# Differential attention: squares written to a small SBUF tile, scaling and turn of seven heads one step later

## The chip, the core and the metric

The kernel runs on one core of one Trainium2 chip. The metric is the device time of one execution in microseconds (us), the median over repeated runs. Five engines matter: TensorE (PE, matmuls and transposes; PEld is its weight load), VectorE (DVE), ScalarE (ACT), GpSimd (POOL) and SyncE (SP, which issues most DMAs).

## What is computed

A trunk of two decoder layers on 512 tokens of width 1024. Each layer is a half-step SwiGLU feed-forward block, a token mixer, a cross-attention into 256 memory tokens and a second feed-forward block, each followed by a layer norm. The mixer of layer 0 is differential attention; only this stage is touched by the change. Cut to its core:

```python
q, k, v = split(x @ w_qkv, 3)          # 8 heads; q, k: two maps of 64; v: 128 wide
q, k = rope(q), rope(k)
for each head, each block of 128 queries:
    p = softmax(mask(q[c] @ k[c].T * 64**-0.5))   for c in (0, 1)
    o = (p[0] - lam * p[1]) @ v
o = o * rsqrt(mean(o**2, axis=-1) + eps) * subln_g * (1 - lam_init)
return o @ w_o
```

The mean of squares in the next-to-last line runs over the 128 values of one head and one token.

## The kernel before

**Precision.** Products are formed from pairs of tiles, a rounded high part and the low rest, so most products are three matmuls (`mm3`) and most results are split in two by ACT (copy, high part) and DVE (subtract, low part).

**Two strands.** `diff_attention` weaves two generators. `da_main` projects queries, keys and values head by head and ends with the first half of the output projection (`to_tokens` over heads 0 to 3). `da_side` runs the attention itself in steps: with 4 blocks of 128 queries (`NT`) and 8 heads there are 32 pairs (head h, block i), and step s = 4h + i starts pair (h, i). `weave` hands out units of the side between matmuls of the main strand: each unit has a weight (`W_SC`, `W_T`, `W_O`, `W_E`), and the next unit comes once matmuls worth 900 ns (`GAP`) times the weight of the one before have been put out. When the main strand has ended, the rest of the side follows without matmuls of the main strand in between; then the second half of the output projection runs.

**One step.** In step s the side does, in this order:

- `da_scores` for the pair of step s: four matmuls into two PSUM tiles (one for each map, 128 x 128(i+1)), then on DVE the masked minimum (L1076) and on ACT the exponential with its sum (L1079), both at high priority. Called SC.i below.
- `da_mix` for the pair one step back (DVE, L1088 to L1090), which joins the two maps.
- `da_turn` for the pair two steps back: i+1 transposes on PE into one PSUM tile (L489), split on ACT and DVE (L120, L121). Called T.i.
- `da_out` for the pair three steps back: the product with v into the PSUM tile `po` (L1111, L1112). Called O.i. Two blocks share one `po` tile, which is taken at O.0 or O.2 and read out after O.1 or O.3: ACT copies one part of it to `o` (L1117), DVE adds the other (L1118), and ACT squares the two blocks of `o`, summing each row into `sq` (L1121). The squares themselves are of no use; they are written back into the `po` bank. After O.3 POOL turns the sums into the factors `f` (L1128 to L1131).
- `da_scale` (ACT, L1137: four instructions on `o`), five steps after the head's last pair (`LS` = 5), and one step later `da_turn_out`: four transposes of `o` on PE (L489, `pt<-ident,o`) and a split into `oT` on ACT (L125) and DVE (L126). Called scale and turn-out.

So in the steady state a head's scale stands in step SC.0 of the head two further on, after T.2 and O.1 of the next head, and its turn-out in the step SC.1, after T.3 and O.2 and ahead of SC.2.

**PSUM.** Besides the two tiles of the projections (`mm`), six banks serve the side: three tags (px, py, yz) of two buffers each. `aux` hands the tags out in rotation, one call after another. A cycle of four steps makes 15 calls, a multiple of three: in order SC.0 (two), T.2, SC.1 (two), T.3, the `po` tile of O.2 and O.3, turn-out, SC.2 (two), T.0, SC.3 (two), T.1, the `po` tile of O.0 and O.1. So every third of these shares two buffers: the second tile of SC.3, for one, has the same tag as the second tile of SC.2 and the `po` tile of O.2.

**Order.** Each engine runs its instructions in an order fixed when the program is built. On PE it is here the order of the strands. On the other engines an instruction can stand ahead of its place in the text where its operands were expected earlier.

Of the kernel before, what the change touches and what calls it, by code (L numbers as in the profile page):

```python
# [12 lines left out]
AF = mybir.ActivationFunctionType  # L13
# [4 lines left out]
P = 128  # L18
D = 1024
S = 512  # L20
NT = S // P
# [7 lines left out]
DA_H = 8  # L29
# [7 lines left out]

V_FIRST, LEAD, GAP = 6, 6000, 900
W_SC, W_T, W_O, W_E = (1.1, 1.4, 1.8, 2.2), (0.5, 0.7, 0.9, 1.1), (0.4, 0.8, 0.6, 1.1), (0.6, 0.8)
LM, LT, LO, LS = 1, 2, 3, 5  # L40
HALVES = (slice(0, DA_DK), slice(DA_DK, P))

FFN_TURNS = (((0, 1, 2), ()), ((3, 4), (0, 1)), ((5, 6), (2, 3)), ((7, 8), (4, 5)), ((9, 10), (6, 7)))
# [66 lines left out]
class Trunk:  # L110
# [75 lines left out]
    def mm(self, name):  # L186
        return self.mmp.tile([P, S], F32, tag="mm", name=name)
# [914 lines left out]
    def da_out(self, st, i):  # L1102
        nc = self.nc
        if i == 0:
            st["o"], st["sq"] = self.tmp("o", (P, NT, P)), self.small("sq", (P, NT))
        if i % 2 == 0:
            st["po"] = self.aux("po").rearrange("p (i s e) -> p i s e", i=2, s=2)
        a, o, po, mm = st.pop(("a", i)), st["o"], st["po"], nc.tensor.matmul
        for j in range(i + 1):
            v = st["v"][j][:, st["h"] % 2]  # L1110
            mm(po[:, i % 2], a[0][:, j], v, start=j == 0, stop=False)  # L1111
            mm(po[:, i % 2, 0], a[1][:, j], v[:, 0], start=False, stop=j == i)  # L1112
        if i % 2 == 0:
            return
        o2 = o[:, i - 1 : i + 1]
        with self.tc.high_priority():
            nc.scalar.copy(o2, po[:, :, 1])  # L1117
            nc.vector.tensor_tensor(o2, o2, po[:, :, 0], ALU.add)  # L1118
        sq = st["sq"]
        for i in range(i - 1, i + 1):  # L1120
            nc.scalar.activation(  # L1121
                po[:, 0, 0], o[:, i], AF.Square, scale=float(P**-0.5), accum_out=sq[:, i : i + 1]
            )
        if i < NT - 1:
            return

        f, G, s0 = self.small("f", (P, NT)), nc.gpsimd, st["sm"][:, :, 0]
        G.tensor_scalar(f, s0, EPS, None, ALU.mult)  # L1128
        G.tensor_tensor(f, f, s0, ALU.mult)
        G.tensor_tensor(f, f, sq, ALU.add)  # L1130
        G.tensor_tensor(f, f, self.mhalf, ALU.pow)  # L1131
        st["f"] = f
# [40 lines left out]
    def da_side(self):  # L1173

        n = DA_H * NT
        for s in range(n + LS + 2):
            h, i = divmod(s, NT)
            if s < n:
                while h >= len(self.heads) or self.clock < self.heads[h][0] + LEAD:
                    yield WAIT  # L1180
                self.da_scores(self.heads[h][1], i)
                yield W_SC[i]
            h, i = divmod(s - LM, NT)
            if 0 <= s - LM < n:
                self.da_mix(self.heads[h][1], i)
            h, i = divmod(s - LT, NT)
            if 0 <= s - LT < n:
                self.da_turn(self.heads[h][1], i)
                yield W_T[i]
            h, i = divmod(s - LO, NT)  # L1190
            if 0 <= s - LO < n:
                while len(self.heads[h][1]["v"]) < NT:
                    yield WAIT
                self.da_out(self.heads[h][1], i)
                yield W_O[i]
            h, i = divmod(s - LS, NT)
            if 0 <= s - LS < n and i == NT - 1:
                self.da_scale(self.heads[h][1])
                yield W_E[0]
            h, i = divmod(s - LS - 1, NT)  # L1200
            if 0 <= s - LS - 1 < n and i == NT - 1:
                self.oT[h] = self.da_turn_out(self.heads[h][1])
                yield W_E[1]

    def diff_attention(self, layer, ln):
        self.low_keys = [self.pair("low") for i in range(2)]
# [367 lines left out]

    def mixer(self, layer, ln):
        if layer == 0:
            bufs = dict(low=4, rt=2, a=4, p=6, o=2, qk=8, _x=0, v=4, oT=11, mask=1)
            with self.other_pools(), self.phase_pool(("v", "v"), "rt", **bufs):
                self.diff_attention(layer, ln)
            self.close_side()  # L1580
        else:
            self.later = ExitStack()
            self.later.enter_context(self.stage_pools(4, dict(raw=2), ("wh", "wl", "mem", "p", "raw")))
            self.to_w(self.later)
            self.kvp = self.later.enter_context(self.pool("kv"))
            bufs = dict(p=4, pw=1, gb=2, _x=0, pooled=16, sq=1)
            with self.phase_pool(("gb", "gb"), "sq", **bufs):
                side = self.pool_mixer(layer, ln)
                with self.tc.high_priority():
                    self.load_memory()  # L1590
                w = self.a["xa_wkv"][layer]
                raws = [self.raw_cols(w, c) for c in (0, D)]
                self.pool_bias()
                next(side)
                self.kv, self.keys, self.kv_bufs = [], [], 10
                self.weave(self.early_kv(layer, ln, 2, raws), side, 850, 8500)
            self.close_side()
# [46 lines left out]
```

## Time and profile before

| | us |
|---|---|
| median of 3 runs (lowest, highest) | 1926.35 (1923.81, 1928.33) |
| the profiled execution, its own time | 1925.08 |
| span of that execution | 1923.3 |
| PE busy | 1892.8 (98%) |
| DVE busy | 1563.6 (81%) |
| ACT busy | 1023.1 (53%) |
| POOL busy | 319.7 (17%) |

The span runs from the first to the last instruction that the profiler recorded; the execution's own time has 1.78 us more around it. Differential attention lies between about 335 and 570 us of the span, the part with the side strand between 371 and 563 us. A line of the profile's timeline gives start, duration, engine, line of the kernel, operation and operands, and in brackets the idle time of the engine just before and what ended it. In a list of waits the three numbers are the total, how many times, and the longest.

### The profile page before, as it was taken

Reading aid. Unit: us, or ns where it says so; the run is one execution under the profiler, and the core shown is the slowest. Engines: PE = TensorE matmul, PEld = TensorE weight load, DVE = VectorE, ACT = ScalarE, POOL = GpSimd, SP = SyncE. Lnnn points to the kernel's source line nnn. Section 1 sums busy time; section 2 is a strip of 40 time slices with the busy share of each in tenths; the row PEclk is TensorE's granted clock in tenths of the full one; section 3 lists DMA queues with packets and bytes.
Section 4 is the critical chain, followed back from the end, with each engine's and each line's share of the span. In section 5 each row is a group of like instructions: output and inputs, shape, how many; then the busy total and the mean of one; then the engine's idle time right before and its main releaser. Section 6 shows DMA issues by size and latency. Waiting matters only on the chain.

```text
span 1923.3 us, 32450 instructions
## 1 busy us (share of the span) xinstructions
PE 1892.8 (98%) x13050; PEld 1737.6 (90%) x13050; DVE 1563.6 (81%) x2263; ACT 1023.1 (53%) x1580; POOL 319.7 (17%) x278
## 2 busy tenths in 40 slices
PE   8999999999999999999999999999999999999998
PEld 7999998888878888999998999999899889999997
DVE  6888989888967558889888988898787568898886
ACT  6555554567755435645554655455455436555553
POOL 2112121111210001221220311212130012111210
PEclk9999999999999999999999999999999999999999
DMA  9978772322124317977785587778334337877861
GB/s 237 221 169 187 166 148 77 91 66 88 61 94 154 110 66 193 181 179 162 144 194 175 108 179 166 179 163 184 111 132 132 132 88 160 173 170 168 185 133 55
DMA packets 246742, 277.94 MB, mean 145 GB/s; under 512 B 8256, under 2 KB 212544, under 8 KB 246592
## 3 DMA queue, kind: packets, MB, share of 16 engines
q0 software_dynamic: 92928, 92.29, 31.2%
q1 hardware_dynamic: 153664, 183.59, 29.3%
q8 instruction: 102, 1.67, 0.4%
q14 instruction: 48, 0.39, 0.1%
HBM read 273.75 MB, written 2.10 MB: 143 GB/s over the span
## 4 chain that ended last, share of the span: by engine, by line
PE 78%; DVE 13%; ACT 4%; DMA 2%; issue 2%; POOL 1%; SPq 0%; DVEq 0%; ACTq 0%; POOLq 0%
PE x L205 7%; PE x L206 7%; PE x L207 7%; PE z L207 4%; PE z L206 4%; PE z L205 4%; PE ps L205 4%; PE ps L207 4%; PE ps L206 4%; DVE wl L121 2%; PE px L205 2%; PE px L207 2%; PE px L206 2%; DMA ra<-in_ffn_w_in_dram 2%; PE y L207 2%
## 5 line engine op out<-in xcount | busy, mean ns | idle before, releaser
L666 POOL DMA_DIRECT2D ra<-in_ffn_w_in_dram x132 | 170.8, 1317 | 987.0 <-DVE wl L121 802.6
L120 ACT CAST wh<-ra 128x1024 fp32r<-128x1024 f32 x184 | 193.4, 1053 | 216.7 <-PE x L206 68.1
L121 DVE TENSOR_TENSOR wl<-ra,wh 128x1024 fp32r<-128x1024 f32 x184 | 223.7, 1221 | 72.8 <-ACT wh L120 72.2
L120 ACT CAST wh<-rc 128x1024 fp32r<-128x1024 f32 x136 | 143.0, 1053 | 116.9 <-PE x L206 41.6
L205 PE MATMUL x<-xe,wh 128*128 128x256 f32 x704 | 195.0, 277 | 0.0
L206 PE MATMUL x<-xe,wh 128*128 128x256 f32 x704 | 194.8, 277 | 0.0
L207 PE MATMUL x<-xe,wl 128*128 128x256 f32 x704 | 194.8, 277 | 0.0
L121 DVE TENSOR_TENSOR wl<-rc,wh 128x1024 fp32r<-128x1024 f32 x136 | 164.8, 1221 | 28.2 <-ACT wh L120 27.8
L120 ACT CAST wh<-b 128x1024 fp32r<-128x1024 f32 x112 | 117.8, 1052 | 128.3 <-PE x L206 65.6
L121 DVE TENSOR_TENSOR wl<-b,wh 128x1024 fp32r<-128x1024 f32 x112 | 136.9, 1222 | 39.4 <-ACT wh L120 39.1
L205 PE MATMUL x<-xh,wh 128*128 128x256 f32 x544 | 151.1, 278 | 0.0
L206 PE MATMUL x<-xl,wh 128*128 128x256 f32 x544 | 150.6, 277 | 0.0
L207 PE MATMUL x<-xh,wl 128*128 128x256 f32 x544 | 150.6, 277 | 0.0
L206 PEld LDWEIGHTS x<-xe,wh 128*128 128x128 f32 x704 | 132.5, 188 | 1.4
L205 PEld LDWEIGHTS x<-xe,wh 128*128 128x128 f32 x704 | 132.2, 188 | 1.3
L207 PEld LDWEIGHTS x<-xe,wl 128*128 128x128 f32 x704 | 132.2, 188 | 0.0
L121 DVE TENSOR_TENSOR wl<-raw,wh 128x1024 fp32r<-128x1024 f32 x64 | 82.8, 1298 | 42.9 <-ACT wh L120 42.2
L206 PEld LDWEIGHTS x<-xl,wh 128*128 128x128 f32 x544 | 102.5, 188 | 0.7
L205 PEld LDWEIGHTS x<-xh,wh 128*128 128x128 f32 x544 | 102.1, 188 | 0.7
L207 PEld LDWEIGHTS x<-xh,wl 128*128 128x128 f32 x544 | 102.2, 188 | 0.0
L207 PE MATMUL y<-xh,wl 128*128 128x256 f32 x352 | 98.5, 280 | 1.2 <-DVE wl L121 0.5
L205 PE MATMUL z<-xh,wh 128*128 128x256 f32 x352 | 97.6, 277 | 1.2 <-ACT xh L120 0.8
(429 smaller groups left out, 6265.7 us busy)
## 6 DMA issues: line engine op xcount, KB each, us to landing
ra<-in_ffn_w_in_dram POOLq DMA_DIRECT2D x132, 512.0 KB, 6.9
rc<-in_ffn_w_in_dram SPq DMA_DIRECT2D x88, 512.0 KB, 5.7
b<-in_ffn_w_out_dram SPq DMA_DIRECT2D x76, 512.0 KB, 4.7
ra<-in_ffn_w_in_dram SPq DMA_DIRECT2D x44, 512.0 KB, 5.0
rc<-in_ffn_w_in_dram POOLq DMA_DIRECT2D x44, 512.0 KB, 7.6
raw<-in_xa_wkv_dram SPq DMA_DIRECT2D x16, 1024.0 KB, 5.5
raw<-in_da_w_qkv_dram SPq DMA_DIRECT2D x16, 512.0 KB, 5.2
raw<-in_xa_wq_dram SPq DMA_DIRECT2D x8, 1024.0 KB, 5.2
```

Source lines behind the costliest of these rows:

```text
L120: self.nc.scalar.copy(hi, src),
L121: self.nc.vector.tensor_sub(lo, src, hi.bitcast(F32)),
L205: mm(out, w[0], x[0], start=start, stop=False, skip_group_check=again)
L206: mm(out, w[0], x[1], start=False, stop=False, skip_group_check=again)
L207: self.last_mm = mm(out, w[1], x[0], start=False, stop=stop, skip_group_check=again)
L666: nc.gpsimd.dma_start(t, source(*block), accum_op=ALU.add)
```

## The change

It has two parts. In `da_out` ACT writes the squares to a new SBUF tile `squares` (128 x 128, one buffer) and not into the first block of the `po` bank; the sums still go to `sq`. In `da_side` the distance `LS` becomes a pair: 6 steps for heads 0 to 6 and 5, as before, for head 7. So scale and turn-out of seven heads move one step on. With the turn-out its call for a PSUM tile moves in the rotation; the order of a cycle becomes SC.0 (two), T.2, SC.1 (two), T.3, `po` of O.2, SC.2 (two), T.0, turn-out, SC.3 (two), T.1, `po` of O.0. The loop loses its last step, in which nothing was done; the count of instructions stays the same.

```diff
-LM, LT, LO, LS = 1, 2, 3, 5
+LM, LT, LO, LS = 1, 2, 3, (6, 5)
...
-        sq = st["sq"]
+        sq, squares = st["sq"], self.tmp("squares", (P, P))
         for i in range(i - 1, i + 1):
             nc.scalar.activation(
-                po[:, 0, 0], o[:, i], AF.Square, scale=float(P**-0.5), accum_out=sq[:, i : i + 1]
+                squares, o[:, i], AF.Square, scale=float(P**-0.5), accum_out=sq[:, i : i + 1]
             )
...
         n = DA_H * NT
-        for s in range(n + LS + 2):
+        for s in range(n + LS[1] + 1):
...
-            h, i = divmod(s - LS, NT)
-            if 0 <= s - LS < n and i == NT - 1:
-                self.da_scale(self.heads[h][1])
-                yield W_E[0]
-            h, i = divmod(s - LS - 1, NT)
-            if 0 <= s - LS - 1 < n and i == NT - 1:
-                self.oT[h] = self.da_turn_out(self.heads[h][1])
-                yield W_E[1]
+            for h in range(DA_H):
+                e = s - (h * NT + NT - 1 + LS[h == DA_H - 1])
+                if e == 0:
+                    self.da_scale(self.heads[h][1])
+                    yield W_E[0]
+                if e == 1:
+                    self.oT[h] = self.da_turn_out(self.heads[h][1])
+                    yield W_E[1]
...
-            bufs = dict(low=4, rt=2, a=4, p=6, o=2, qk=8, _x=0, v=4, oT=11, mask=1)
+            bufs = dict(low=4, rt=2, a=4, p=6, o=2, qk=8, _x=0, v=4, oT=11, mask=1, squares=1)
```

## The prediction

> **What bounds the kernel now.** I read the head of the page first, then PE's busy time in the stretch of the side strand (365 to 565 us), then the list of PE's waits in 335 to 575 us.
>
> ```profile
> span 1923.3 us, 32450 instructions
> PE 1892.8 (98%) x13050; PEld 1737.6 (90%) x13050; DVE 1563.6 (81%) x2263; ACT 1023.1 (53%) x1580; POOL 319.7 (17%) x278
> 365.00:565.00 200.00, 192.89 (x1141) 166.78 (x1139) 170.30 (x428) 133.91 (x360) 35.16 (x47) 1.00 0.25 79
> PE pt L489 <- DVE p L1090: 2.6, 2, 1.4
> PE sc L1070 <- ACT po L1121: 1.5, 2, 0.8
> PE pt L489 <- ACT o L1137: 1.1, 1, 1.1
> PE sc L1070 <- ACT qk L1057: 0.9, 2, 0.7
> PE po L1112 <- DVE a L121: 0.6, 1, 0.6
> ```
>
> PE is busy for 98% of the span. In this stretch (length, then busy time of PE, PEld, DVE, ACT, POOL) it stands still for 200 - 192.89 = 7.1 us, and the five lines below account for 6.7 of that. So no rearrangement of the side strand can win more than about 7 us, 0.37% of the kernel, and 1.4 of that is the longer of two waits for L1090, at the first head, before any scale or turn-out. What an edit to DVE or ACT is worth is only what it takes off these waits, or adds to them. They lie here:
>
> ```profile
> 416.21 0.33 PE L1070 MATMUL sc<-qk 128*128 128x128 f32 x1 [0.65 <-ACT qk L1057]
> 440.81 0.33 PE L1112 MATMUL po<-v,a 128*128 128x128 f32 x1 [0.64 <-DVE a L121]
> 485.77 0.33 PE L1070 MATMUL sc<-qk 128*128 128x128 f32 x1 [0.78 <-ACT po L1121]
> 489.10 0.55 PE L489 MATMUL pt<-ident,p 128*128 128x128 f32 x3 [1.21 <-DVE p L1090]
> 499.07 0.44 PE L1070 MATMUL sc<-qk 128*128 128x384 f32 x1 [0.68 <-ACT po L1121]
> 560.77 0.33 PE L489 MATMUL pt<-ident,o 128*128 128x128 f32 x1 [1.11 <-ACT o L1137]
> ```
>
> The 485.77 and 499.07 rows are SC.0 and SC.2 of head 5, waiting for a bank in which ACT still writes squares. The 560.77 row is the turn-out of head 7, when the main strand has run out.
>
> **Part 1: squares to SBUF.** No instruction is removed or added; 32 squares change their target, and a `po` bank is free after DVE's add (L1118) instead of after the second square (L1121). Around 485 us ACT and DVE ran as follows.
>
> ```profile
> 479.23 0.69 ACT L125 ACTIVATE oT<-pt,subg 128x512 fp32r<-128x512 f32 x1
> 479.81 0.61 ACT L1079 ACTIVATE p<-p,mx 128x384 f32<-128x384 f32 x1
> 481.14 0.17 DVE L1088 RECIPROCAL rc<-sd 128x1 f32<-128x1 f32 x1 [0.44 <-ACT p L1079]
> 484.06 0.41 DVE L1118 TENSOR_TENSOR o<-o,po 128x256 f32<-128x256 f32 x1
> 485.33 0.26 ACT L1121 ACTIVATE po<-o 128x128 f32<-128x128 f32 x1
> 487.14 0.40 ACT L1137 ACTIVATE o<-o,f 128x128 f32<-128x128 f32 x1 [0.77 <-POOL f L1131]
> 487.45 0.71 ACT L1079 ACTIVATE p<-p,mx 128x512 f32<-128x512 f32 x1
> 494.03 0.41 DVE L1118 TENSOR_TENSOR o<-o,po 128x256 f32<-128x256 f32 x1
> 498.62 0.28 ACT L1121 ACTIVATE po<-o 128x128 f32<-128x128 f32 x1
> ```
>
> With the bank free at 484.47 (484.06 + 0.41) PE need not wait at 485.77 - 0.78 = 484.99; with the second bank free at 494.44 it need not wait at 498.39. Upper bound: 0.78 + 0.68 = 1.46 us won. But the first wait is followed 3.3 us later by the 1.21 at 489.10 for DVE (L1090), and a PE that comes 0.78 earlier waits there so much longer, unless DVE comes earlier too. So the first is worth between 0 and 0.78; which, part 2 says. The second has no later wait behind it until the end of the stage: 0.68.
>
> The squares themselves get longer. Their rows and the nearest ones with the same 128 x 128 shape and an SBUF target:
>
> ```profile
> L1121 ACT ACTIVATE po<-o x32: 259/282/283, 392.2 to 558.4; 128x128 f32<-128x128 f32 x32
> L1137 ACT ACTIVATE o<-o,f x32: 385/392/406, 405.1 to 561.2; 128x128 f32<-128x128 f32 x32
> ```
>
> 392 - 282 = 0.11 us each (bounds: 0, if the target does not matter, and 0.11); I take 0.11. All 32 make 3.5 us of ACT time. ACT is busy for 133.91 of 200 us here, so 66 us of idle time hide it, except at the tail, where PE waits for a chain through two squares: 2 x 0.11 = 0.22 lost. Without that cover the 3.5 us would be the cost (a rival below). [...]
>
> **Part 2: scale and turn-out one step later.** I followed the units of the side strand through the weave by their weights. Scale and turn-out together weigh 1.4, that is 1.26 us of main-strand matmuls: SC.1, T.3, O.2, and then SC.2, T.0, O.3 of each cycle come up to that much earlier against the projections; SC.3 and all behind it stay. At the end, O.3 of head 7 now precedes the turn-out of head 6.
>
> The scale itself will hardly move. At 487.14 the first scale of head 3 ran on ACT before the exponentials of SC.3 of head 5 (487.45), some three units ahead of its place in the text: it is put where ACT would otherwise be idle, once `f` is expected. One step later in the text its place in that gap stays, so the wait for POOL (0.77 here) stays too. I cost this move at 0; the bounds are 0 and what the first rival wins.
>
> The turn-out does move on PE, and with it L125 (0.69) and L126. At 479.23 L125 runs just before the exponentials that DVE waits for at 481.14 (0.44 idle). Behind SC.2 it no longer delays them, so DVE reaches L1090 up to 0.44 earlier, and of the first 0.78 I count 0.44. Sum of the two PSUM waits: 0.44 + 0.68 = 1.1 us won (bounds 0.68 and 1.46).
>
> At the tail:
>
> ```profile
> 554.92 0.60 PE L489 MATMUL pt<-ident,o 128*128 128x128 f32 x4
> 556.05 0.28 PE L1111 MATMUL po<-v,a 128*128 128x256 f32 x1
> 557.11 0.38 ACT L1117 COPY o<-po 128x256 f32<-128x256 f32 x1 [0.87 <-PE po L1112]
> 560.31 1.28 ACT L1137 ACTIVATE o<-o,f 128x128 f32<-128x128 f32 x4 [1.49 <-POOL f L1131]
> ```
>
> O.3 of head 7 begins at 556.05, one group of three matmuls and the turn-out (from 554.92) later than it could: 1.1 us. ACT waited for it (0.87). Put ahead, the chain copy, add, squares, `f`, scale starts about 1.0 earlier, less 0.22 for longer squares: 0.8 of the 1.11 at 560.77 (bounds 0, if DVE's adds and the turn-out of head 6 get in between, and 1.11).
>
> The move has a price in banks. The second tile of SC.3 shares two buffers with its tag's last two tiles. Those were the second tile of SC.2 and `po` of O.2; now they are the tile of T.0, only one step old, and `po`, read out by the add after O.3. For heads 2, 4 and 6 the rows give the second SC.3 tile on PE, the DVE split of T.0 and the add:
>
> ```profile
> 432.38 0.50 PE L1070 MATMUL sc<-qk 128*128 128x512 f32 x1
> 433.37 0.29 DVE L121 TENSOR_TENSOR a<-pt,a 128x128 fp32r<-128x128 f32 x1
> 434.36 0.41 DVE L1118 TENSOR_TENSOR o<-o,po 128x256 f32<-128x256 f32 x1
> ...
> 481.16 0.40 PE L1070 MATMUL sc<-qk 128*128 128x512 f32 x1
> 482.45 0.28 DVE L121 TENSOR_TENSOR a<-pt,a 128x128 fp32r<-128x128 f32 x1
> ...
> 524.67 0.40 PE L1070 MATMUL sc<-qk 128*128 128x512 f32 x1
> 525.13 0.28 DVE L121 TENSOR_TENSOR a<-pt,a 128x128 fp32r<-128x128 f32 x1
> 525.34 0.41 DVE L1118 TENSOR_TENSOR o<-o,po 128x256 f32<-128x256 f32 x1
> ```
>
> At these times the split ends 1.28, 1.57 and 0.74 us after PE wants the bank: 3.6 us. T.0 comes up to 1.26 earlier, which leaves 0.02 + 0.31 + 0. I take 0.3 (bounds 0 and 3.6). Queued behind a waiting SC.3 tile are the projections, since PE keeps its order: such a wait is lost in full. I found no other tile that is late for its successor in the new rotation. The new SBUF tile lies behind the others of its stage, so no address of another tile moves. Queues of DMAs are not passed: neither part issues one, and POOL's four instructions per head stay behind O.3.
>
> **Sum.** -1.1 - 0.8 + 0.3 = -1.6 us. Against the profiled execution's 1925.08 that is 1923.5; that execution lay 1.27 below the median of the runs, so as a median 1926.35 - 1.6 = 1924.7 us.
>
> **Rivals.**
>
> First, the scale does come off the wait for `f`. Then heads 1 to 6 no longer hold ACT, and behind it DVE:
>
> ```profile
> ACT o L1137 <- POOL f L1131: 7.8, 7, 2.3
> 405.07 0.40 ACT L1137 ACTIVATE o<-o,f 128x128 f32<-128x128 f32 x1 [2.32 <-POOL f L1131]
> 407.46 0.42 DVE L121 TENSOR_TENSOR a<-pt,a 128x256 fp32r<-128x256 f32 x1 [2.16 <-ACT a L120]
> ```
>
> DVE would win some 2 us at 407, and the waits at 416 (0.65 and 0.20), 440.81 (0.64) and the rest of 489.10 (0.8) would go: 2.3 more, -3.9 in all, 1922.4 us. For it: ACT waits there 7 times, 7.8 us in all. Against it: the scale stands ahead of its place already.
>
> Second, slower: the bank of the second SC.3 tile decides. If the tile is given the `po` bank, PE waits for the add: 2.39 (432.38 to 434.77), 3.31 (481.16 to 484.47) and 1.08 (524.67 to 525.75), 6.8 us for three heads, net -1.9 + 6.8 = +4.9, 1931.2 us; with the tile of T.0 at the old times it is +1.7, 1928.0. It decides once T.0 and O.3 do not come earlier on DVE along with PE: their splits are queued on a DVE that is busy for 170.30 of 200 us, and the turn-out's split is now queued between. Against it: the high priority of the splits and of the add. [...]
>
> Third, the 3.5 us of longer squares fall on the path: squares stand before exponentials on ACT, for which DVE waits (481.14). Net +1.9, 1928.2 us.
>
> Fourth, nothing comes of it: the freed banks only move the two waits to DVE's L1090 and to a split, and the tail keeps its wait: 1926.3 us.
>
> **How the numbers follow.** Forecast 0.40, first rival 0.17, second 0.27, third 0.08, fourth 0.08. A change of 0.2% (3.85 us, about the spread of the runs shown) can just be told from none. Below 1922.5 lie most of the first rival and the lower end of the forecast (0.13 + 0.09); above 1930.2 most of the second and part of the third rival (0.21 + 0.04). So faster 0.22, same 0.53, slower 0.25. The range: from 1921.0, below the first rival by half of what runs spread, to 1932.5, above the second with the `po` bank. The forecast's own range is 1922.5 to 1927.
>
> **What would show it.** Right: no wait for L1121 in PE's list; a wait at head 7's turn-out under 0.5 us; ACT's squares near 0.39 us; the first scale still ahead of SC.3's exponentials, with a wait for L1131. Wrong: PE waits at L1070 of the 512-wide tiles for L121 or L1118 (second rival); no ACT wait for L1131 and none on PE near 416 and 441 (first); DVE waits for L1079 grown by more than 2 us (third).

## The result, and the profile after

| | before | after |
|---|---|---|
| median of 15 runs each (lowest, highest), us | 1926.61 (1923.81, 1930.73) | 1933.15 (1929.72, 1936.48) |
| ratio after to before, 95% interval | | 1.0033 (1.0026 to 1.0040) |
| span of the profiled execution, us | 1923.3 | 1931.4 |
| first score matmul to the wait at head 7's turn-out, us | 371.79 to 560.77 = 188.98 | 374.03 to 568.18 = 194.15 |

The changed kernel is slower by 0.33%, 6.5 us. Of the 8.1 us between the two spans 5.2 lie in the stage of the side strand. 2.2 lie ahead of it and are no part of the change: a second profile of the same program (e6_after_again below) begins that stage at 372.98, and the profiles of the other kernels begin it anywhere from 371.07 to 373.37.

The head of the page after, and PE's list of waits in 335 to 585 us:

```profile
span 1931.4 us, 32441 instructions
PE 1897.7 (98%) x13050; PEld 1741.3 (90%) x13050; DVE 1564.1 (81%) x2263; ACT 1023.2 (53%) x1580; POOL 320.4 (17%) x278
PE pt L489 <- DVE p L1090: 3.7, 2, 2.4
PE sc L1070 <- DVE oT L126: 2.7, 1, 2.7
PE pt L489 <- ACT o L1137: 1.1, 1, 1.1
PE sc L1070 <- ACT qk L1057: 1.1, 3, 0.7
```

No wait for L1121 is left. In its place stands one that the kernel before does not have, for the turn-out's split (L126). Of the two for the join of the maps (L1090) the one at the first head is 1.36 as before, and the other is 2.36 where it was 1.21. On PE's timeline:

```profile
491.25 0.45 PE L1070 MATMUL sc<-qk 128*128 128x128 f32 x1 [2.67 <-DVE oT L126]
522.38 0.63 PE L489 MATMUL pt<-ident,p 128*128 128x128 f32 x4 [2.36 <-DVE p L1090]
568.18 0.33 PE L489 MATMUL pt<-ident,o 128*128 128x128 f32 x1 [1.11 <-ACT o L1137]
```

The first is the second tile of SC.0 of head 5. In the new rotation it takes the bank of head 2's turn-out, six calls back. Why is that bank late? The other engines around it, with some rows between left out, and last the same L126 in the kernel before:

```profile
486.21 0.67 ACT L125 ACTIVATE oT<-pt,subg 128x512 fp32r<-128x512 f32 x1
486.24 1.30 POOL L1030 TENSOR_TENSOR rt<-rt,ropeS 128x512 f32<-128x512 f32 x1 [8.24 <-DVE rt L1028]
486.58 2.04 DVE L121 TENSOR_TENSOR wl<-raw,wh 128x1024 fp32r<-128x1024 f32 x1
487.49 1.18 POOL L1130 TENSOR_TENSOR f<-f,sq 128x4 f32<-128x4 f32 x1
488.54 0.68 DVE L1076 CUSTOM_DVE_ANT_0 p<-sc,mask 128x512 f32<-128x512 f32 x1
488.75 1.04 POOL L1131 TENSOR_TENSOR f<-f,mhalf 128x4 f32<-128x4 f32 x1
489.82 1.28 ACT L1137 ACTIVATE o<-o,f 128x128 f32<-128x128 f32 x4 [2.94 <-POOL f L1131]
490.36 0.74 DVE L126 SCALAR_TENSOR_TENSOR oT<-pt,subg,oT 128x512 fp32r<-128x512 f32 x1
491.00 0.71 ACT L1079 ACTIVATE p<-p,mx 128x512 f32<-128x512 f32 x1
492.54 0.17 DVE L1088 RECIPROCAL rc<-sd 128x1 f32<-128x1 f32 x1 [1.44 <-ACT p L1079]
```

```profile
479.95 0.75 DVE L126 SCALAR_TENSOR_TENSOR oT<-pt,subg,oT 128x512 fp32r<-128x512 f32 x1
```

ACT's half of the split, which DVE's half reads, is done at 486.88 (486.21 + 0.67). DVE's half starts 3.5 us later: `wl`, 2.04 us long, the two minima of SC.3 and an instruction of the main strand (L1031, 0.68) stand ahead of it. Before, the same instruction ran at 479.95, between the minima of SC.2 and of SC.3, and no tile waited for it. At the same place ACT now holds SC.3's exponentials back for the first scale, which waits 2.94 us for POOL (0.77 before), and DVE stands idle for them (1.44).

For the second wait the order on DVE went the other way. It is the 512-wide T.3 of head 5, whose scores began at 509.38:

```profile
510.60 0.31 ACT L1121 ACTIVATE squares<-o 128x128 f32<-128x128 f32 x1 [2.53 <-DVE o L1118]
510.91 0.67 ACT L125 ACTIVATE oT<-pt,subg 128x512 fp32r<-128x512 f32 x1
511.61 0.75 DVE L126 SCALAR_TENSOR_TENSOR oT<-pt,subg,oT 128x512 fp32r<-128x512 f32 x1 [1.05 <-ACT oT L125]
512.28 0.68 DVE L1076 CUSTOM_DVE_ANT_0 p<-sc,mask 128x512 f32<-128x512 f32 x1
```

Here L126 stands ahead of the minima and waits for ACT, so that 1.05 + 0.75 us pass on DVE ahead of the scores that T.3 needs. That these 1.8 us make the 2.36 is argued from the order; no run shows it alone.

Is that all of the loss? The stage in one stretch each, of the kernel before and the kernel after (length, busy time of PE, PEld, DVE, ACT, POOL; the third number from the end is PE's granted clock):

```profile
371.79:560.77 188.98, 182.19 (x1096) 158.69 (x1094) 162.23 (x413) 128.91 (x352) 33.42 (x46) 1.00 0.25 78
```

```profile
374.03:568.18 194.15, 184.68 (x1092) 160.33 (x1091) 162.54 (x413) 128.38 (x352) 32.92 (x46) 0.98 0.24 74
```

PE stands still for 6.79 us before and 9.47 after: 2.68 more, about half of the 5.17 by which the stage grew. The other 2.49 are busy time of PE, on the same matmuls (a few records are missing from each trace, so the counts differ). DVE and ACT do the same work as before.

The loss is made in one part of the stage. The stage of the profile after begins 2.24 us later than that of the profile before, and SC.2 of head 4 still begins only 1.99 later (477.49 against 475.50), though by then two heads have had their turn-out one step later. SC.0 of head 7 begins 8.22 later (536.50 against 528.28), and there the loss is complete; 0.8 us of it is won back by the end of the stage.

Where PE's busy time comes from:

```profile
491.25:495.00 3.75, 3.75 (x12) 3.06 (x12) 2.01 (x5) 2.66 (x7) 0.43 (x2) 0.50 0.48 185
495.00:498.00 3.00, 3.00 (x13) 2.57 (x12) 2.96 (x10) 2.46 (x7) 0.88 (x1) 0.62 0.00 0
```

Right behind the 2.67 wait PE works at 0.50 of its clock for 3.75 us and at 0.62 for another 3.0: 3.75 x 0.50 + 3.00 x 0.38 = 3.0 us of its work is lost, some 0.5 more than the busy time grew.

### The profile page after: what moved, and what is told of

It reads as the page before. It is cut to its first block, busy times and chain, and to the rows that moved or that the text cites. A ratio compares the mean times of both kernels' runs of the same rounds, so it can differ in the third digit from the quotient of the medians.

```text
span 1931.4 us, 32441 instructions
## 1 busy us (share of the span) xinstructions
PE 1897.7 (98%) x13050; PEld 1741.3 (90%) x13050; DVE 1564.1 (81%) x2263; ACT 1023.2 (53%) x1580; POOL 320.4 (17%) x278
## 3 DMA queue, kind: packets, MB, share of 16 engines
q8 instruction: 102, 1.67, 0.4%
## 4 chain that ended last, share of the span: by engine, by line
PE 77%; DVE 14%; ACT 4%; issue 2%; DMA 2%; POOL 1%; SPq 0%; DVEq 0%; ACTq 0%; POOLq 0%
PE x L206 7%; PE x L205 7%; PE x L207 7%; PE z L207 4%; PE z L206 4%; PE z L205 4%; PE ps L205 4%; PE ps L207 3%; PE ps L206 3%; DVE wl L121 3%; PE px L205 2%; PE px L207 2%; PE px L206 2%; PE y L207 2%; PE pz L207 2%
## 5 line engine op out<-in xcount | busy, mean ns | idle before, releaser
L121 DVE TENSOR_TENSOR wl<-ra,wh 128x1024 fp32r<-128x1024 f32 x184 | 223.7, 1220 | 72.0 <-ACT wh L120 71.5
L121 DVE TENSOR_TENSOR wl<-rc,wh 128x1024 fp32r<-128x1024 f32 x136 | 164.6, 1219 | 29.7 <-ACT wh L120 29.3
L121 DVE TENSOR_TENSOR wl<-b,wh 128x1024 fp32r<-128x1024 f32 x112 | 136.7, 1221 | 40.8 <-ACT wh L120 40.8
L121 DVE TENSOR_TENSOR wl<-raw,wh 128x1024 fp32r<-128x1024 f32 x64 | 83.0, 1300 | 43.0 <-ACT wh L120 42.2
```

The costliest lines, as they stand in the source:

```text
L121: self.nc.vector.tensor_sub(lo, src, hi.bitcast(F32)),
```

## The experiments

Ratios are to the kernel before, with 95% intervals, and need not be the quotient of the two medians given; "stage" is the stretch in the last row of the table above, 188.98 before and 194.15 after. Where an edit adds lines, the line numbers behind it shift: L1092, L1140, L1133 and L1123 are then the L1090, L1137, L1131 and L1121 of the kernel before.

### Which of the two parts?

**e1_squares_only** makes the first part alone: squares to `squares`, scale and turn-out in their old steps.

```diff
+        sq, squares = st["sq"], self.tmp("squares", (P, P))
-                po[:, 0, 0], o[:, i], AF.Square, ...
+                squares, o[:, i], AF.Square, ...
```

> The kernel before with the squares in SBUF and scale and turn-out where they were. Theory (the move of the turn-out costs, the squares win): PE no longer waits for L1121 (0.78 and 0.68 before), the rest stays; 0.7 to 1.5 us below before, about 1925.5, and no wait of PE over 1.4 us. Rival (the longer way of the squares to SBUF delays the factors f and with them everything): 3 us or more above before, 1930 or more.

Measured: 1927.86 against 1927.35 us, ratio 1.0006 (0.9997 to 1.0015); stage 188.97.

```profile
490.28 0.55 PE L489 MATMUL pt<-ident,p 128*128 128x128 f32 x3 [2.22 <-DVE p L1090]
515.83 0.66 PE L489 MATMUL pt<-ident,p 128*128 128x128 f32 x4 [0.60 <-DVE a L121]
```

The two waits for L1121, 0.78 and 0.68, are gone, but the 1.21 for L1090 has become 2.22 and a new 0.60 for L121 stands behind it: 1.46 us removed, 1.61 added. Neither the gain nor the loss that was expected came. The program's instructions stand in the same order as before on every engine; only the waits differ.

**e2_later_only** makes the second part alone, with the squares in the bank.

```diff
-LM, LT, LO, LS = 1, 2, 3, 5
+LM, LT, LO, LS = 1, 2, 3, (6, 5)
...
+            for h in range(DA_H):
+                e = s - (h * NT + NT - 1 + LS[h == DA_H - 1])
```

> The change without its first part: squares go to the bank as before, scale and turn-out of seven heads one step later. Theory (the later turn-out holds a bank that SC.0 wants): PE waits at an SC.0 tile for L126 by 2 us or more, as in the changed kernel, and the time is 5 to 9 us above before, about 1933. Rival (the loss needs both parts): within 2 us of before, 1925 to 1929.

Measured: 1933.00 against 1927.35 us, ratio 1.0030 (1.0019 to 1.0042); stage 194.24.

```profile
488.38 0.44 PE L1070 MATMUL sc<-qk 128*128 128x128 f32 x1 [2.64 <-DVE oT L126]
519.52 0.63 PE L489 MATMUL pt<-ident,p 128*128 128x128 f32 x4 [2.04 <-DVE p L1090]
```

The whole loss comes with the later steps, and so does the wait for L126. The target of the squares neither makes nor spares it. A third wait, 1.42 us for another split (L121), stands at SC.2 of head 5 (500.73).

### Scale or turn-out?

**e4_turn_later** leaves the scale in its old step and moves the turn-out alone (squares in SBUF from here on, but for one kernel).

```diff
+                if e == (0 if h == DA_H - 1 else -1):
                     self.da_scale(self.heads[h][1])
...
                 if e == 1:
                     self.oT[h] = self.da_turn_out(self.heads[h][1])
```

> The changed kernel with the scale of heads 0 to 6 back in its old step and only the turn-out one step later. Theory (the turn-out's place costs): the wait of SC.0 for L126 stays, 4 to 8 us above before, about 1932. Rival (the scale's place costs, by its wait for f): within 2 us of before.

Measured: 1932.26 against 1927.35 us, ratio 1.0030 (1.0018 to 1.0043); stage 194.98.

```profile
489.18 0.30 PE L1070 MATMUL sc<-qk 128*128 128x128 f32 x1 [2.64 <-DVE oT L126]
520.81 0.63 PE L489 MATMUL pt<-ident,p 128*128 128x128 f32 x4 [2.27 <-DVE p L1090]
```

**e5_scale_later** does the opposite: scale one step later, turn-out behind it in its old step.

```diff
                 if e == 0:
                     self.da_scale(self.heads[h][1])
...
+                if e == (1 if h == DA_H - 1 else 0):
                     self.oT[h] = self.da_turn_out(self.heads[h][1])
```

> The changed kernel with the turn-out of heads 0 to 6 back in its old step, right behind the scale, which stays one step later than before. Theory (the turn-out's place costs): no wait of PE for L126, time within 2 us of the squares-only kernel, 1924 to 1927. Rival (the scale's place costs): 4 us or more above before, 1930.5 or more.

Measured: 1928.75 against 1927.35 us, ratio 1.0004 (0.9995 to 1.0013); stage 189.24, no wait for L126. The median is within 2 us of the squares-only kernel, as expected, and above the 1927 that was named with it. The two kernels divide the loss: it is the turn-out's. The scale's place in the text does nothing, as the prediction had it.

**e10_turn_two_later** moves the turn-out one step further still, behind O.0 and ahead of the next SC.0, away from SC.3's minima.

```diff
+                if e == (1 if h == DA_H - 1 else 2):
                     self.oT[h] = self.da_turn_out(self.heads[h][1])
```

> The changed kernel with the turn-out of heads 0 to 6 yet another step later, behind O.0 and just ahead of SC.0, the smallest step. Theory (the place ahead of SC.3, whose minima and exponentials are the longest, is what costs): no wait for L126 over 1 us and no T.3 wait over 1.5 us; 3 us or more below the changed kernel, 1930 or less. Rival (any later place costs, since the bank is then held beside SC.0): the time of the changed kernel or more, 1932 or more.

Measured: 1930.76 against 1926.78 us, ratio 1.0023 (1.0014 to 1.0032); stage 193.77. Both sizes were missed, since the time fell between them. The wait for L126 is gone, and others have taken its place:

```profile
465.96 0.33 PE L1070 MATMUL sc<-qk 128*128 128x128 f32 x1 [1.39 <-ACT qk L1057]
516.08 0.39 PE L1070 MATMUL sc<-qk 128*128 128x256 f32 x1 [1.90 <-DVE mx L1076]
```

So the bank that SC.0 takes over is where the later turn-out's cost shows, and at most a part of what makes it.

### Is it the place of the split on DVE?

**e3_turn_split_first** is the changed kernel with the turn-out's split at high priority.

```diff
-        self.split_scaled(hi, lo, pt, self.subg)
+        with self.tc.high_priority():
+            self.split_scaled(hi, lo, pt, self.subg)
```

> The changed kernel with the two instructions of the turn-out's split (L125, L126) at high priority; by this L126 of head 3 stands on DVE before the minima of SC.3 of head 5, not after them. Theory (two separate harms: the bank of the turn-out held for SC.0 of head 5, and L126 ahead of SC.3's minima for head 6): the wait of 2.67 at SC.0 is gone, the wait of some 2.3 at T.3 of head 6 stays; 2 to 4 us below the changed kernel, 1929 to 1931. Rival (one harm, a late DVE, that comes out at one place or another): a wait of 2 us or more appears elsewhere near 485 to 500 us, and the time stays within 1.5 us of the changed kernel, 1931.5 to 1934.5.

Measured: 1932.07 against 1926.78 us, ratio 1.0029 (1.0017 to 1.0040); stage 193.76.

```profile
489.38 0.30 PE L1070 MATMUL sc<-qk 128*128 128x128 f32 x1 [1.43 <-DVE oT L126]
497.06 0.66 PE L489 MATMUL pt<-ident,p 128*128 128x128 f32 x4 [1.19 <-DVE a L121]
521.31 0.63 PE L489 MATMUL pt<-ident,p 128*128 128x128 f32 x4 [2.98 <-DVE p L1090]
```

(The SC.3 of head 5 and the T.3 of head 6 of this expectation are those of heads 4 and 5 here, and its L126 is that of head 2.) The theory of two separate harms fell: the wait for L126 lost 1.24 us, a new wait for L121 took 1.19, and the time is not 2 us below the changed kernel. The third wait is no sign either way, since a second profile of the changed kernel (e6_after_again below) has 2.98 there too. The time is the rival's, though its new wait is shorter than the 2 us that it named. One late DVE, which comes out at one place or another, is the reading that fits. The stage in one stretch:

```profile
373.37:567.13 193.76, 183.46 (x1092) 158.07 (x1090) 162.54 (x413) 127.96 (x352) 32.89 (x46) 1.00 0.24 74
```

The clock stayed whole here and PE stood still for 10.30 us instead, and the time is that of the changed kernel within 1.1 us. So the loss does not need the low clock, which is one of the forms in which it is paid.

**e6_after_again** is the changed kernel once more.

```diff
-V_FIRST, LEAD, GAP = 6, 6000, 900
+V_FIRST, LEAD, GAP = 6, 6000, 900.0
```

> The changed kernel a second time (900 is written as 900.0, the program is the same), for the granted clock after its long waits. If a wait of 2.4 to 2.7 us on PE lowers the clock by chance of where it falls in time: the same two long waits, but the clock falls to half at another place, for another length, or not at all. If it is tied to the wait: half clock for 6.8 us from about 2 us into the wait for L126 again.

One run of 1933.58 us, stage 195.75, with the clock halved behind both long waits, and not for the double length behind the first. The waits are 2.66 and 2.98 us. Two profiles of one program so differ by 1.6 us in the stage, and smaller differences between two stages alone say nothing.

### What holds ACT: the scale ahead of the exponentials

The scale waits for POOL with SC.3's exponentials queued behind it, in the kernel before as in the changed one. **e7_scale_behind** keeps the old steps, with squares in SBUF, and puts each head's scale behind the last exponentials of that SC.3 in the order of issue.

```diff
-                nc.scalar.activation(
+                self.last_exp = nc.scalar.activation(
                     p[m], p[m], AF.Exp, ...
...
+        if i == NT - 1:
+            self.scale_after = self.last_exp
...
-        for i in range(NT):
-            self.nc.scalar.activation(o[:, i], o[:, i], AF.Copy, scale=f[:, i : i + 1])
+        with self.tc.issue_after(self.scale_after.ins):
+            for i in range(NT):
+                self.nc.scalar.activation(o[:, i], o[:, i], AF.Copy, scale=f[:, i : i + 1])
```

> The kernel with the squares in SBUF and scale and turn-out in their old steps, but each scale put on ACT behind the exponentials of the last SC.3. It tests the first rival of the prediction directly. If ACT's waits for f set the pace of DVE near 405 and 437: those waits (7.8 us in all before) fall below 1 us, the waits of PE near 416 and 441 shrink by 1 us or more, 1 to 3 us below the squares-only kernel, about 1925. If DVE's own work sets it: time within 1 us of the squares-only kernel.

Measured: 1923.16 against 1926.78 us, ratio 0.9981 (0.9972 to 0.9990); stage 184.84. ACT's wait for `f` in 365 to 575 us, and what is left of PE's waits behind the first head:

```profile
ACT o L1140 <- POOL f L1133: 3.0, 4, 1.5
485.41 0.55 PE L489 MATMUL pt<-ident,p 128*128 128x128 f32 x3 [1.67 <-DVE p L1092]
510.63 0.66 PE L489 MATMUL pt<-ident,p 128*128 128x128 f32 x4 [0.24 <-DVE a L121]
556.26 0.33 PE L489 MATMUL pt<-ident,o 128*128 128x128 f32 x1 [1.11 <-ACT o L1140]
```

ACT waits 3.0 us for `f` where it waited 7.8 (under 1 was expected), and PE's waits near 416 and 441 are gone. This is what the first rival of the prediction said, by an edit that does move the scale. Its third item did not come: the wait for the join of the maps, 1.21 before, is 1.67.

**e11_psum_scale_behind** makes that edit on the kernel before, squares in the bank.

```diff
+        with self.tc.issue_after(self.scale_after.ins):
...
                 po[:, 0, 0], o[:, i], AF.Square, ...
```

> The kernel before, with its squares in the PSUM bank and scale and turn-out in their old steps, but each head's scale put behind the last exponentials of the SC.3 that it stood ahead of. Theory (the scale, hoisted into a wait for f, holds ACT and behind it DVE; the bank that the squares hold costs little once DVE is not late): nearly the whole gain of the same edit with squares in SBUF (-3.6 us), so 2.0 to 3.6 us under the kernel before, with waits of PE for L1121 of under 1.5 us in sum. Rival (the free bank is what the scale's place makes usable): the two waits for L1121 stay and the gain is under 1.5 us.

Measured: 1923.09 against 1926.64 us, ratio 0.9979 (0.9970 to 0.9988); stage 185.10.

```profile
482.82 0.33 PE L1070 MATMUL sc<-qk 128*128 128x128 f32 x1 [0.28 <-ACT po L1123]
486.14 0.55 PE L489 MATMUL pt<-ident,p 128*128 128x128 f32 x3 [1.22 <-DVE p L1092]
495.82 0.44 PE L1070 MATMUL sc<-qk 128*128 128x384 f32 x1 [0.36 <-ACT po L1123]
```

The whole gain without touching the squares. Their two waits have shrunk to 0.28 and 0.36 by themselves.

**e12_after_scale_behind** makes it on the changed kernel, turn-out one step later.

```diff
 LM, LT, LO, LS = 1, 2, 3, (6, 5)
...
+        with self.tc.issue_after(self.scale_after.ins):
```

> The changed kernel in full, turn-out one step later, but each head's scale put behind the last exponentials of the SC.3 that it stood ahead of. Theory (the later turn-out is dear because its split comes due while ACT waits for f and DVE is late): 1927.5 or less, no wait of PE over 1.0 us for the turn-out's split (L126). Rival (the later turn-out costs by itself, by its place in the rotation of banks between T.0 and SC.3 and its split among the minima of SC.3): 1929.5 or more, and a wait of PE for L126 of 1.5 us or more stays.

Measured: 1927.87 against 1926.64 us, ratio 1.0005 (0.9995 to 1.0014); stage 188.95. The time missed both sizes, by 0.4 and 1.6 us; the wait is the rival's:

```profile
485.75 0.74 DVE L126 SCALAR_TENSOR_TENSOR oT<-pt,subg,oT 128x512 fp32r<-128x512 f32 x1
486.63 0.30 PE L1070 MATMUL sc<-qk 128*128 128x128 f32 x1 [2.65 <-DVE rc L1090]
516.02 0.63 PE L489 MATMUL pt<-ident,p 128*128 128x128 f32 x4 [1.86 <-DVE p L1092]
```

The view names the reciprocal (L1090 here is L1088 before), but the bank is the turn-out's, and its split ends at 486.49, 0.14 us ahead of the matmul.

**e13_both_mended** adds the high priority of e3_turn_split_first to that.

```diff
+        with self.tc.high_priority():
+            self.split_scaled(hi, lo, pt, self.subg)
```

> The changed kernel in full, turn-out one step later, with each head's scale behind the last exponentials of its SC.3 and the turn-out's split (L125, L126) at high priority. Theory (what is left of the later turn-out's cost is the place of its split on DVE, behind SC.3's minima, for which SC.0's second tile waits 2.65 us): that wait falls to 1.4 us or less and the time to 1926.0 or less. Rival (DVE is late there anyhow, and the wait comes out at another place, as it did when the split alone was put first): 1927.0 or more, with a new or longer wait of PE for L121 or for the join of the maps of 1 us or more.

Measured: 1927.69 against 1927.28 us, ratio 1.0005 (0.9996 to 1.0014); stage 190.53.

```profile
484.26 0.30 PE L1070 MATMUL sc<-qk 128*128 128x128 f32 x1 [1.40 <-DVE oT L126]
492.94 1.03 PE L489 MATMUL pt<-ident,p 128*128 128x128 f32 x4 [2.77 <-DVE a L121]
```

The wait for L126 falls as the theory asked, and 2.77 us for L121 appear behind it: the rival again.

Four of these kernels make a square:

| ratio to the kernel before (stage, us) | turn-out in its old step | turn-out one step later |
|---|---|---|
| scale ahead of SC.3's exponentials | 1.0006 (188.97) | 1.0033 (194.15) |
| scale behind them | 0.9981 (184.84) | 1.0005 (188.95) |

The later turn-out costs 0.0027 and 0.0024 in the two rows, some 5 us; the scale's place is worth 0.0025 and 0.0028 in the two columns. Within the intervals the effects add up, so the later turn-out does not cost by way of the scale's wait for `f`, however large that wait looks at 489.82: ACT's waits for `f` are 10.8 us in all in the kernel after and 2.1 in e12, and the later turn-out costs about the same in both rows. It costs by itself.

The version that beats both kernels is the kernel before with the scale behind the exponentials, 0.2% faster, with or without the squares in SBUF.

## Why the prediction was wrong

**The step that failed is the price of the turn-out's move in banks**, "I take 0.3 (bounds 0 and 3.6)", with the 0.44 us that the move was to win at L125. The prediction sought the late bank at the second tile of SC.3 and wrote that it found no other tile late for its successor. Of the SC.3 tiles only one waits in any of these kernels, in e4_turn_later, for 0.39 us. The late one is the second tile of SC.0, which takes the turn-out's own bank; the prediction moved the turn-out on PE and did not ask what stands ahead of its split on DVE at the new time. L126 has no high priority, and one step later it comes due beside SC.3's minima, `wl` and a busy POOL. Moving it off that bank (e10) or ahead of the minima (e3, e13) mostly moves the wait. Measured, the term was about +5 us (0.0024 to 0.0030 of the time, in e2, e4 and the square) and not +0.3 - 0.44.

**The second rival** had the sign and the kind of wait (a bank behind a split that is queued on DVE), on the wrong tile. Its size was luck: the 6.8 us of its sum are waits of three SC.3 tiles for the add, and no run has one of these.

**The freed banks.** The waits for L1121 did vanish. The 1.1 us (bounds 0.68 and 1.46) did not come: e1 shows 0 for both, with 2.22 for 1.21 at L1090. The prediction warned that a PE which comes 0.78 earlier may only wait longer there, and gave the second wait its full worth because no later wait stood behind it; a new one, 0.60 for L121, did. On this part the fourth rival is right.

**Longer squares.** In the kernel after:

```profile
L1121 ACT ACTIVATE squares<-o x32: 294/310/313, 394.5 to 565.8; 128x128 f32<-128x128 f32 x32
```

0.310 against 0.282 us: 0.03 each, where 0.11 was taken from the scale's row. The sign is right, and the size, 0.9 us of ACT over 32, is too small to matter to the end.

**The scale's place.** That the later step in the text would leave the scale ahead of SC.3's exponentials, at no cost or gain, holds (e5, 1.0004). (The prediction calls that SC.3 head 5's; it is head 4's.) The gain of the first rival was there as well, by another edit. That 3.6 us (e7, e11) are near the 3.9 worked out is luck: 1.6 of the 3.9 were the forecast's own terms, which did not come, and the scale was given 2.3.

**The tail.** 0.8 of the 1.11 was to go, and nothing went. From T.3 to O.3 of head 7 the time fell by 0.46 us only (551.70 to 556.05 before, 559.11 to 563.00 after), and the turn-out that was put behind O.3 came back on ACT, between the two squares:

```profile
564.93 0.31 ACT L1121 ACTIVATE squares<-o 128x128 f32<-128x128 f32 x1 [0.49 <-DVE o L1118]
565.26 0.69 ACT L125 ACTIVATE oT<-pt,subg 128x512 fp32r<-128x512 f32 x1
565.84 0.30 ACT L1121 ACTIVATE squares<-o 128x128 f32<-128x128 f32 x1
```

This is the lower bound that the prediction named, with ACT in the part of DVE.

**Not in the prediction at all** were the halved clock and the place of the long `wl`, both below.

What stays open: why DVE as a whole falls behind once the turn-out comes later, beyond the two places shown. No instruction was added, and no single reordering that was tried gives the 5 us back. One piece is in sight and untested: a `wl` of 1.97 to 2.04 us begins 2.6 to 3.8 us ahead of an L126 in all eight profiles with a later turn-out, and its like (1.95 to 2.02) some 10 us ahead of the next L126 in the five with the old one.

## What to carry to other kernels

When a step moves, place its instructions anew on every engine and ask there what is ahead of each and what is behind; a bank that was free at the old time says nothing about the new one. Where a producer is late as a whole, as DVE here, freeing one buffer (e1) or raising one split (e3) moved the wait to the next thing that it owed; a square of two edits, as above, shows cheaply whether two suspects are one. The scale, put ahead into a gap on ACT, waited there with SC.3's exponentials queued behind it (7.8 us for `f` in all, 3.0 once it stood behind them): on an engine that is busy for 53% of the span that cost this kernel 3.6 us (e7).

## What the runs showed of the hardware

**PE's clock at half behind waits of 1.9 to 3.0 us.** In the kernel after the granted clock is 0.50 behind the 2.67 us for L126 (above). Besides that, the granted clock falls to half near the end of a wait of 1.9 to 3.0 us, or right behind it, in the profiles of seven other runs. For e13_both_mended, behind its 2.77 us:

```profile
488.00:492.60 4.60, 2.17 (x12) 1.51 (x10) 4.54 (x10) 2.91 (x10) 1.28 (x1) 1.00 0.00 0
492.60:496.00 3.40, 3.06 (x10) 2.60 (x11) 3.37 (x12) 3.15 (x10) 0.00 (x0) 0.56 0.02 5
```

It is not so each time: e1 with 2.22, e3 with 2.98 and the first 2.64 of e4 kept the full clock, as did the kernel after behind its 2.36, and of two runs of one program one had 6.8 us of half clock behind the first wait, the other 3.4 behind each. The stretches at half clock in the clock's record are 3.41 us long or twice that (6.827 us in the kernel after), those at full clock between them are whole multiples of the same length (477.866 us in the kernel after is 140 times 3.413), so in these records the clock changed on a grid of 3.413 us.

The half clock went, but for one case, with how much of a wait fell into one interval of that grid. Between 365 and 585 us of the 13 profiles PE stood still for 1.87 us or more of an interval ten times, and nine times the next interval was at half clock (in the kernel after 1.87 us, from 487.04 to 490.46); the exception is e3 (1.94 us, from 519.36 to 522.78). After an interval at full clock with 1.62 us or less of standing still it never was. The 2.22 of e1 fell into two intervals, 1.16 and 1.06 us, the first 2.64 of e4 as 1.37 and 1.27, and the 2.36 of the kernel after as 1.16 and 1.20. From these lengths, a stretch of 3.41 us at 0.50 takes up to 1.7 us of PE's work (an estimate: 3.41 / 2).

**`wl` on DVE beside POOL's L1030: 2.04 us, and 1.22 with POOL at rest.** In the kernel after, with POOL at rest and with DVE at rest respectively:

```profile
478.77 1.22 DVE L121 TENSOR_TENSOR wl<-raw,wh 128x1024 fp32r<-128x1024 f32 x1
436.62 0.20 POOL L1130 TENSOR_TENSOR f<-f,sq 128x4 f32<-128x4 f32 x1 [7.82 <-ACT squares L1121]
```

At 486.58 the same `wl` takes 2.04 us, where POOL had begun L1030 at 486.24 (rows above). Estimated from these rows as standing still until POOL is done at 487.54, it would end 1.22 us later, at 488.76; it ended at 488.62. And L1130, begun at 487.49, takes 1.18 us and ends with it, at 488.67. Beside L126, which has one input in PSUM, L1130 takes its 0.20 us (at 511.94). At 486.58 `wl` so took 0.8 us more of DVE; the one at 406.31, beside L1131 (begun at 406.22), took its 1.22. The kernel before has such a `wl` too, 1.95 us at 510.20, where POOL had begun L1030 at 509.78, and the 30 of them in the stage take 28.15 us before and 27.56 after: the change did not add one, it brought it ahead of L126.
